# A diffusion layer on one Trainium2 core: norm rows turned by a small matmul before they are written, their reads tied in the queue, and the first operand splits of the up projection behind the last copy of the Fourier part

## The chip, the core and the metric

The kernel runs on one core of one Trainium2 chip. The metric is the device time of one execution in microseconds (us). The text names the engines as the profile does: PE is TensorE (matmuls), DVE VectorE, ACT ScalarE, POOL GpSimd, SP SyncE, whose queue issues nearly all DMA transfers here. "Granted clock" (PEclk) is the share of full TensorE clock that the chip gave: 1.0 is 2.4 GHz, 0.5 is 1.2 GHz.

## The reference, cut to what matters

One layer of a diffusion backbone, in float32, over 2048 tokens of width 1024. `mix` is an output projection of two halves joined: 512 channels of gated retention, and 512 channels of a 2-D Fourier transform.

```python
mix = jnp.concatenate([ret, fourier_mix(f)], axis=-1) @ w_out
x = x + gt_a * rms_norm(mix, g_mix_post)
h_ffn = modulate(rms_norm(x, g_ffn_pre), sh_f, sc_f)
u = h_ffn @ w_up                                    # width 2 * 2816
u = conv3_along_each_row_of_64_tokens(u) + conv_b
a, b = jnp.split(u, 2, axis=-1)
ffn = (jax.nn.silu(a) * b) @ w_down
x = x + gt_f * rms_norm(ffn, g_ffn_post)
```

`rms_norm` divides by the root of the mean square over the 1024 channels: one number for each token, so three norms are to be taken here for each of the 2048 tokens (after `mix`, before the feed-forward part, after it).

## The kernel before, in words

Activations lie with the channels on the 128 partitions and 512 tokens in a row; b = 0 to 3 counts the blocks of 512 tokens, n = 0 to 7 the tiles of 128 channels. Every float32 operand is split in two parts: `split` has ACT cast the high part (L82) and DVE subtract it to get the low part (L83). A product of two split operands is three matmuls (`mm3`, L90, L91, L92).

**Output projection.** `mix_mm(b, n)` runs 32 steps t = 8b + n. The Fourier half is already in SBUF as a tile M; ACT copies it into a PSUM tile `psmix` as a seed (`seed_mix`, L996) two steps ahead (SEEDS = 2), and 12 matmuls with the weights `wr` and the split retention rows `rt` add the other half. ACT copies the sum back into M (L1007) and squares it into `accm`. `load_r` loads and splits the rows `rt` of the next block.

**Norms.** `sum_cols` sums squares over the partitions by 4 matmuls with a column of ones (tile `pc`, L160); DVE scales them (`rp`, L128) and POOL takes the power (L129). The result is 128 x 4: a token is a partition. To multiply a tile that has tokens along the row, the kernel needs it as a row on all partitions. It goes there in one of two ways: `bcast_row` (4 matmuls `pb`, L86, and a copy by ACT, L146), or through DRAM: `row_out` (L133) writes the 128 x 4 tile into a vector of 512, and `row_in` (L138) reads it back, the same 512 numbers on every partition. Eight rows go through DRAM: n1, n2, n3 (before the feed-forward, blocks 1 to 3), m2, m3 (after `mix`) and three of the last norm (`row_f`). Rows `n` come from the sums `accx`, rows `m` from `accm`.

**Between the two.** `mix_post` scales M by the row, adds the residual and squares into `accx`; `x2_cols` and `x2_rows` make the row n. `t_first` and `t_second` then make the right operands of the up projection for blocks 0 and 1 (`h_val`, L1040, and splits `b` and `t`; the last of them are needed some 10 us into the up pass). The dictionary `steps` says after which step t each of these is written in the code.

**Feed-forward.** Two passes over pairs of blocks, each an up projection (tiles `psu`, `psf`) and a down projection (`psd`). Weights come as `ur` (L1152), are summed into `us` for a Strassen-like scheme and split into `u_a`, `u_s`. Blocks 2 and 3 of `mix_post` and `x2_cols` run as a generator, `rest_of_mix`, some of it after each pair of tiles of the first up pass, as "background". At the end of each up pass four tiles `xn` (blocks 1 and 3) are scaled by row n1 or n3.

A scheduler puts the instructions of the program in an order for each engine; an instruction under `keep_in_program_order` stays behind those that were written ahead of it. Each engine then runs its own list strictly in order, and SP issues its DMAs so too.

Of the kernel before, what the change touches and what calls it, by code (L numbers as in the profile page):

```python
# [14 lines left out]
P = 128  # L15
NT = 2048
D = 1024
KT = 8
# [26 lines left out]
J0 = (0, 11), (0,)  # L45
UPJ = [j for k in range(1, KH) for j in (k, k + KH)]
KO = list(range(1, KH)) + [0]
RS = 8, 4
SEEDS = 2
CPAD, APAD, PPAD = 48, 48, 8  # L50
WFN = 272
# [4 lines left out]
def kern(tc, A, out):  # L56
    nc = tc.nc

    with ExitStack() as es:
# [15 lines left out]
        def pmt(shape, name):  # L75
            return psp.tile(shape, F32, tag="pm", name=name, bufs=2)
# [1 line left out]
        def cst(shape, name, p=cp):  # L78
            return p.tile(shape, F32, tag=name, name=name)

        def split(hi, lo, src):
            nc.scalar.copy(hi, src)  # L82
            nc.vector.tensor_tensor(lo, src, hi.bitcast(F32), op=ALU.subtract)  # L83

        def mm(ps, l, r, start, stop):
# [43 lines left out]
            nc.gpsimd.tensor_tensor(o, t[:, 0:n], mhalf[:, 0:n], op=ALU.pow)  # L129

        def row_out(rc, n, name, eng=None):
            d = dp.tile([n * P], F32, tag="row_" + name, name="row_" + name)
            (eng or nc.sync).dma_start(d.rearrange("(i p) -> p i", p=P), rc)  # L133
            return d

        def row_in(rt, d, n, name, eng=None):
            rr = rt([P, n * P], "rr_" + name)
            (eng or nc.sync).dma_start(rr, bass.AP(tensor=d.tensor, offset=d.offset, ap=[[0, P], [1, n * P]]))  # L138
            return rr

        def bcast_row(rt, rc, n, name):
# [870 lines left out]
        def mix_cols(b):  # L1012
            rcm[b] = cst([P, 4], f"rcm{b}", po_)
            sum_cols(accm[b], rcm[b], 4, po_)
            if b > 1:
                rowm[b] = row_out(rcm[b], 4, f"m{b}")

        def mix_rows(b):
            if b < 2:
# [3 lines left out]

        def x2_cols(b):
            sum_cols(accx[b], r2c[:, 4 * b:4 * b + 4], 4, po_)
            if b:
                r2d[b] = row_out(r2c[:, 4 * b:4 * b + 4], 4, f"n{b}")

        def x2_rows(b, eng=None):
            if b > 1 or b in rrn:  # L1030
# [107 lines left out]
        def operands(bb, jobs):  # L1138


            def load(j, one):
                if bb and not one and j in wus:
                    a1, a2, sb = (page([P, KT, P], F32, f"ur{i}") for i in range(3))
                    sa = sump.tile([P, 2, 4, P], F32, tag="sum", name="us")
                    nc.sync.dma_start(a1, A["w_up"][j])
                    nc.sync.dma_start(sa, wus[j][:, 0:2])
                    nc.sync.dma_start(sb, wus[j][:, 2:4].rearrange("p s k c -> p (s k) c"))
                    nc.sync.dma_start(a2[:, 0:4], A["w_up"][j + NJ][:, 4:8])
                    return dict(a11=a1[:, 0:4], a12=a1[:, 4:8], s1=sa[:, 0], s2=sa[:, 1], s4=sb[:, 0:4], s3=sb[:, 4:8], a22=a2[:, 0:4])
                r = [page([P, KT, P], F32, f"ur{i}") for i in range(2)]  # L1150
                for i in range(2):
                    nc.sync.dma_start(r[i], A["w_up"][j + NJ * i])  # L1152
                return dict(a11=r[0][:, 0:4], a12=r[0][:, 4:8], a21=r[1][:, 0:4], a22=r[1][:, 4:8])

            def left_sum(a, o):
                l, r, op = dict(s1=("a21", "a22", ALU.add), s2=("s1", "a11", ALU.subtract),
                                s3=("a11", "a21", ALU.subtract), s4=("a12", "s2", ALU.subtract))[o]
                nc.vector.tensor_tensor(a[o], a[l], a[r], op=op)

            def split_of(a, nme):  # L1160
                w = spt([P, 2, 4, P], f"u_{nme}")
                split(w[:, 0], w[:, 1], a[nme])
                return w

            def gen(nxt):
                held = None
                for i, (j, one) in enumerate(jobs):
                    a = nxt
                    if i + 1 < len(jobs):
                        nxt = load(*jobs[i + 1])  # L1170
                    if one:
                        if held is not None:
                            yield split_of(held, PAIR[6][0])
                            held = None
                        for nme in ONE:
                            yield split_of(a, nme)
                        continue
                    sums = "s1" not in a
                    if sums:
                        sa = sump.tile([P, 2, 4, P], F32, tag="sum", name="us")  # L1180
                        a.update(s1=sa[:, 0], s2=sa[:, 1], s3=a["a21"], s4=sa[:, 1])
                        for o in ("s1", "s2"):
                            left_sum(a, o)
                        if not bb:
                            nc.sync.dma_start(wus[j][:, 0:2], sa)
                    for q, (nme, _) in enumerate(PAIR[:6]):
                        o = dict(s1="s3", a12="s4").get(nme)
                        if sums and o:
                            left_sum(a, o)
                            if not bb:  # L1190
                                nc.sync.dma_start(wus[j][:, ("s4", "s3").index(o) + 2], a[o])
                        yield split_of(a, nme)
                        if q == 1 and held is not None:
                            yield split_of(held, PAIR[6][0])
                    held = a
            return gen(load(*jobs[0]))
# [10 lines left out]
        def at(t, f, *a):  # L1207
            steps.setdefault(t, []).append((f, a))
        for b in range(NB - 1):
            for k in range(4):  # L1210
                at(RS[0] * b + RS[1] * k // 2, load_r, b + 1, k)
        T = {}
        tf, ts = t_first(T, 0), t_second(T, 1)
        T["gen"] = ts
        for b, t in ((0, 9), (1, 17)):
            at(t, mix_cols, b)
            at(t + 1, mix_rows, b)
            for n in range(KT):
                at(t + 2 + n // 2, mix_post, b, n)
            at(t + 6, x2_cols, b)  # L1220
            at(t + 7, x2_rows, b)
        at(27, mix_cols, 2)
        for n in range(KT):
            at(17 + n, next, tf)
        at(26, lambda: up0.append(up_load(0)))
        early = []
        for n in range(4):
            at(28, lambda: early.append(next(up0[0][2])))
        for n in range(12):
            at(26 + n // 2, next, ts)  # L1230
        for t in range(SEEDS):
# [1 line left out]
        for t in range(32):  # L1233
            mix_mm(t // KT, t % KT)
            for f, a in steps.get(t, ()):
                f(*a)


        def rest_of_mix():
            mix_cols(3)  # L1240
            for b in (2, 3):
                mix_rows(b)
                got = mix_load(b, 0)
                yield
                yield
                for n in range(KT):
                    now, got = got, mix_load(b, n + 1) if n + 1 < KT else None
                    mix_post(b, n, now)
                    yield
                for _ in range(XW):  # L1250
                    yield
                x2_cols(b)
                yield

        def conv(y, ps, j):
# [174 lines left out]
        class Norm:  # L1430
# [6 lines left out]
            def f(self, n):  # L1437
                return self.fo[n // 2][:, n % 2]
# [356 lines left out]
```

## Time and profile before

| | |
|---|---|
| device time, median of 3 runs | 2201.43 us (2195.55 to 2203.13) |
| time of the profiled execution | 2195.93 us, of which the span of the trace is 2194.2 |
| mean granted clock | 0.978 |
| PE busy | 2076.4 us, 95% of the span |
| DVE, ACT, POOL busy | 1615.2, 1009.2 and 616.7 us (74%, 46%, 28%) |
| output projection | about 726 to 857 us of the span |
| first up pass, first down pass | 857 to 1311, 1311 to 1521 |
| second up pass, second down pass | 1521 to 1958, 1958 to 2194 |

A row of the timeline gives the start and the length of an instruction or of a run of equal ones, its engine, line, operation and tiles (out<-in), and in brackets how long the engine had stood idle and whom it waited for.

### The profile page before, as it was taken

How to read it: one execution, taken by the hardware profiler on the slowest of the kernel's cores; microseconds unless marked ns; L12 is line 12 of the kernel's file. 1: busy time of each engine (PE TensorE's matmuls, PEld its weight loads, DVE VectorE, ACT ScalarE, POOL GpSimd, SP SyncE). 2: the span in 40 equal slices, each digit the busy share in tenths (PEclk: the TensorE clock that was granted, in tenths of full speed). 3: DMA queues.
4: the chain of work that ended last, by engine and by line, in shares of the span. 5: the costliest groups of instructions: out<-in, count | busy, mean ns of one | idle time of the engine just before them, and what ended most of it. 6: DMA issues, size and time to landing. Idle time of an engine off the chain costs nothing.

```text
span 2194.2 us, 28116 instructions
## 1 busy us (share of the span) xinstructions
PE 2076.4 (95%) x9819; PEld 1711.4 (78%) x9819; DVE 1615.2 (74%) x2346; ACT 1009.2 (46%) x1754; POOL 616.7 (28%) x496
## 2 busy tenths in 40 slices
PE   7899899999899977989989999999999999999996
PEld 3777778888798866778778888887887888878886
DVE  6876877767566387998898886778777777775557
ACT  4342233324444566544545554545555455553441
POOL 4101122323101243242343342021333334331025
PEclk9999999999999988999999999999999999999998
DMA  8676643232562155664564478665355655386653
GB/s 306 213 242 216 192 139 92 100 96 95 146 223 100 52 199 139 183 207 176 183 205 159 154 275 297 218 242 177 135 187 197 185 185 178 135 272 224 200 154 130
DMA packets 202590, 395.20 MB, mean 180 GB/s; under 512 B 31816, under 2 KB 69584, under 8 KB 202448
## 3 DMA queue, kind: packets, MB, share of 16 engines
q1 hardware_dynamic: 194416, 367.07, 51.6%
q0 software_dynamic: 7600, 26.23, 3.3%
q8 instruction: 77, 1.26, 0.2%
q14 instruction: 65, 0.53, 0.1%
q10 hardware_dynamic: 432, 0.11, 0.0%
HBM read 275.33 MB, written 118.00 MB: 179 GB/s over the span
## 4 chain that ended last, share of the span: by engine, by line
PE 56%; DVE 22%; DMA 10%; issue 6%; ACT 3%; POOL 2%; SPq 1%; DVEq 0%; ACTq 0%; POOLq 0%
PE psu L90 8%; PE psu L91 8%; PE psu L92 8%; PE psd L90 5%; PE psd L91 5%; PE psd L92 5%; DMA ur<-in_w_up 2%; DVE u_a L83 2%; DVE y L1259 1%; DVE u_s L83 1%; DVE fd L638 1%; DMA wsum<-in_w_down 1%; DMA adaw<-in_wadaB 1%; PE pada L86 1%; DMA wd<-wsum 1%
## 5 line engine op out<-in xcount | busy, mean ns | idle before, releaser
L83 DVE TENSOR_TENSOR dlo<-draw,dhi 128x1024 fp32r<-128x1024 f32 x154 | 200.3, 1323 | 113.7 <-ACT dhi L82 102.4
L91 PE MATMUL psd<-dlo,dhi 128*128 128x512 f32 (+1 forms) x660 | 247.1, 375 | 2.9 <-DVE dlo L83 2.9
L92 PE MATMUL psd<-dhi,dlo 128*128 128x512 f32 (+1 forms) x660 | 246.2, 375 | 0.0
L1297 POOL TENSOR_TENSOR y<-y,y 128x512 f32<-128x512 f32 x82 | 127.0, 1549 | 388.5 <-DVE y L1260 274.5
L82 ACT CAST dhi<-draw 128x1024 fp32r<-128x1024 f32 x154 | 159.7, 1051 | 162.2 <-PE psd L92 116.5
L90 PE MATMUL psd<-dhi 128*128 128x512 f32 (+1 forms) x660 | 209.4, 375 | 0.6 <-DVE cx L1558 0.6
L91 PE MATMUL psu<-t,u_s 128*128 128x512 f32 x492 | 194.1, 395 | 1.4 <-DVE t L83 1.4
L90 PE MATMUL psu<-t,u_s 128*128 128x512 f32 x492 | 194.9, 396 | 0.0
L92 PE MATMUL psu<-t,u_s 128*128 128x512 f32 x492 | 193.9, 394 | 0.0
L83 DVE TENSOR_TENSOR u_a<-ur,u_a 128x512 fp32r<-128x512 f32 x147 | 139.7, 953 | 61.3 <-ACT u_a L82 60.8
L90 PE MATMUL psu<-b,u_a 128*128 128x512 f32 x424 | 165.6, 391 | 3.1 <-ACT u_a L82 1.9
L91 PE MATMUL psu<-b,u_a 128*128 128x512 f32 x424 | 165.2, 390 | 0.0
L92 PE MATMUL psu<-b,u_a 128*128 128x512 f32 x424 | 165.2, 390 | 0.0
L91 PEld LDWEIGHTS psd<-dlo,dhi 128*128 128x128 f32 x660 | 124.2, 188 | 25.6 <-DVE dlo L83 3.3
L92 PEld LDWEIGHTS psd<-dhi,dlo 128*128 128x128 f32 x660 | 124.2, 188 | 22.3
L90 PEld LDWEIGHTS psd<-dhi 128*128 128x128 f32 x660 | 123.3, 188 | 23.2 <-DVE cx L1558 0.8
L82 ACT CAST u_a<-ur 128x512 fp32r<-128x512 f32 x147 | 90.6, 620 | 103.0 <-PE psu L92 92.3
L1256 ACT ACTIVATE y<-psu,cb,cw 128x512 f32<-128x512 f32 x135 | 104.2, 775 | 19.0 <-DVE psu L1405 13.7
L83 DVE TENSOR_TENSOR u_s<-us,u_s 128x512 fp32r<-128x512 f32 x103 | 84.7, 823 | 38.4 <-ACT u_s L82 38.3
L91 PEld LDWEIGHTS psu<-t,u_s 128*128 128x128 f32 x492 | 94.1, 191 | 22.0 <-DVE t L83 1.9
L90 PEld LDWEIGHTS psu<-t,u_s 128*128 128x128 f32 x492 | 94.1, 191 | 19.9 <-ACT psu L1394 0.9
L92 PEld LDWEIGHTS psu<-t,u_s 128*128 128x128 f32 x492 | 93.8, 191 | 20.0
(438 smaller groups left out, 5313.9 us busy)
## 6 DMA issues: line engine op xcount, KB each, us to landing
ur<-in_w_up SPq DMA_DIRECT2D x74, 512.0 KB, 5.5
draw<-wd SPq DMA_DIRECT2D x88, 256.0 KB, 5.6
draw<-ft SPq DMA_DIRECT2D x88, 256.0 KB, 5.8
ft<-y SPq DMA_DIRECT2D x36, 512.0 KB, 5.5
draw<-in_w_down SPq DMA_DIRECT2D x66, 256.0 KB, 5.1
draw<-fb SPq DMA_DIRECT2D x66, 256.0 KB, 5.3
xt<-in_xT SPq DMA_DIRECT2D x56, 256.0 KB, 4.0
adaw<-in_wadaB SPq DMA_DIRECT2D x24, 512.0 KB, 6.5
```

What stands on the lines that cost most here:

```text
L82: nc.scalar.copy(hi, src)
L83: nc.vector.tensor_tensor(lo, src, hi.bitcast(F32), op=ALU.subtract)
L86: nc.tensor.matmul(ps, l, r, start=start, stop=stop)
L90: nc.tensor.matmul(ps, lhi, rhi, start=start, stop=False, skip_group_check=on)
L91: nc.tensor.matmul(ps, lhi, rlo, start=False, stop=False, skip_group_check=on)
L92: nc.tensor.matmul(ps, llo, rhi, start=False, stop=stop, skip_group_check=on)
L638: tc.keep_in_program_order(nc.vector.tensor_tensor(o_, a_, b_, op=op))
L1256: nc.scalar.activation(y, ps, AF.Identity, bias=cb[:, j:j + 1], scale=cw[:, j, 1:2])
L1259: nc.vector.scalar_tensor_tensor(y3[:, :, 1:64], p3[:, :, 0:63], cw[:, j, 0:1], y3[:, :, 1:64], ALU.mult, ALU.add)
L1297: nc.gpsimd.tensor_tensor(y1, y1, y2, op=ALU.mult)
```

## The change

1. `row_out` first turns the 128 x 4 tile into 4 x 128 by a matmul with the identity (`prow`), DVE copies that out of PSUM (`rowt`), and the DMA writes 4 rows of 128 numbers, where it wrote 512 separate numbers.
2. The reads of `row_in` are tied in program order.
3. `row_out` stands in functions of its own (`mix_out`, `x2_out`), called a step or more after the sums; `rest_of_mix` gets four more yields.
4. `load_r` of block b + 1 stands after steps 8b + 1 to 8b + 4 (before: 8b, 8b + 2, 8b + 4, 8b + 6).
5. `x2_cols` and `x2_rows` stand one step later; the first weights of the up pass (`up_load(0)`) one step earlier.
6. The first four operand splits of the up pass stand two after step 28 and two after step 29, their ACT copies tied; before, all four were written at step 28, free to move.

```diff
-        def split(hi, lo, src):
-            nc.scalar.copy(hi, src)
+        def split(hi, lo, src, tie=False):
+            c = nc.scalar.copy(hi, src)
+            if tie:
+                tc.keep_in_program_order(c)
...
         def row_out(rc, n, name, eng=None):
             d = dp.tile([n * P], F32, tag="row_" + name, name="row_" + name)
-            (eng or nc.sync).dma_start(d.rearrange("(i p) -> p i", p=P), rc)
+            pr = pmt([n, P], "prow")
+            mm(pr, rc, ident, True, True)
+            t = cp.tile([n, P], F32, tag="rowt", name="rowt")
+            nc.vector.tensor_copy(t, pr)
+            (eng or nc.sync).dma_start(d.rearrange("(i p) -> i p", p=P), t)
...
         def row_in(rt, d, n, name, eng=None):
-            (eng or nc.sync).dma_start(rr, bass.AP(...))
+            r = (eng or nc.sync).dma_start(rr, bass.AP(...))
+            tc.keep_in_program_order(r)
...
         def mix_cols(b):
-            if b > 1:
-                rowm[b] = row_out(rcm[b], 4, f"m{b}")
+        def mix_out(b):
+            rowm[b] = row_out(rcm[b], 4, f"m{b}")
...
         def x2_cols(b):
-            if b:
-                r2d[b] = row_out(r2c[:, 4 * b:4 * b + 4], 4, f"n{b}")
+        def x2_out(b):
+            r2d[b] = row_out(r2c[:, 4 * b:4 * b + 4], 4, f"n{b}")
...
-                split(w[:, 0], w[:, 1], a[nme])
+                split(w[:, 0], w[:, 1], a[nme], not bb and len(early) < 4)
...
-                at(RS[0] * b + RS[1] * k // 2, load_r, b + 1, k)
+                at(KT * b + 1 + k, load_r, b + 1, k)
...
-            at(t + 6, x2_cols, b)
-            at(t + 7, x2_rows, b)
+            at(t + 7, x2_cols, b)
+            at(t + 8, x2_rows, b)
+        at(26, x2_out, 1)
         at(27, mix_cols, 2)
+        at(28, mix_out, 2)
...
-        at(26, lambda: up0.append(up_load(0)))
+        at(25, lambda: up0.append(up_load(0)))
         early = []
-        for n in range(4):
-            at(28, lambda: early.append(next(up0[0][2])))
...
             for f, a in steps.get(t, ()):
                 f(*a)
+            if t in (28, 29):
+                early.extend(next(up0[0][2]) for _ in range(2))
...
         def rest_of_mix():
             mix_cols(3)
+            yield
+            mix_out(3)
+            yield
...
                 x2_cols(b)
+                yield
+                x2_out(b)
                 yield
```

The last seeds and the first operand splits in ACT's list, around the last two steps of the output projection; `u_a<-ur` are the splits of the up pass, `psmix<-m` the seed of step 31. Before:

```order
L1007 COPY m_3_5902<-psmix 128x512
L154 ACTIVATE sq<-psmix 128x512
L82 CAST u_a_7299<-ur_7219 128x512
L82 CAST u_a_7302<-ur_7219 128x512
L82 CAST u_a_7305<-ur_7220 128x512
L82 CAST u_a_7308<-ur_7220 128x512
L1041 ACTIVATE h_7311<-h_7311,modB 128x512
L82 CAST t_0_7318<-m_0_5899 128x512
L996 COPY psmix<-m_3_6094 128x512
```

The same place in the changed kernel:

```order
L1014 COPY m_3_5902<-psmix 128x512
L161 ACTIVATE sq<-psmix 128x512
L81 CAST t_0_7310<-m_0_5899 128x512
L1003 COPY psmix<-m_3_6094 128x512
L1014 COPY m_3_5966<-psmix 128x512
L1050 ACTIVATE h_7303<-h_7303,modB 128x512
L1014 COPY m_3_6030<-psmix 128x512
L1050 ACTIVATE h_7304<-h_7304,modB 128x512
L81 CAST b_1_7315<-h_7304 128x512
L81 CAST u_a_7322<-ur_7198 128x512
L81 CAST u_a_7325<-ur_7198 128x512
```

Four splits stood ahead of the last seed; now the seed stands ahead of all of them, and PE's first three `psu` matmuls, which stood ahead of step 31, stand behind it. SP's list at the end of the first up pass, where the row n1 is read (`fb<-y` are stores of the gated tiles, `wu` stores of weight sums, `ur` loads of weights). Now:

```order
L1200 DMA wu_225<-us 128x512
L1161 DMA ur_10345<-in_w_up 128x1024
L1161 DMA ur_10346<-in_w_up 128x1024
L1293 DMA ft_0_194<-y_9864 128x1024
L1194 DMA wu_227<-us 128x1024
L1200 DMA wu_227<-ur_10346 128x512
L1293 DMA fb_0_151<-y_10170 128x512
L144 DMA rr_n_10657<-row_n_7221 128x512
L1200 DMA wu_226<-us 128x512
```

Before, the same read stood in SP's list at the end of the output projection, between the writes of rows n1 and m2 and the first weights:

```order
L133 DMA row_n_7144<-r2c 128x4x1
L1152 DMA ur_7219<-in_w_up 128x1024
L1009 DMA x_2_3_119<-m_3_6030 128x512
L1152 DMA ur_7220<-in_w_up 128x1024
L133 DMA row_m_7263<-rcm_7254 128x4x1
L1009 DMA x_3_3_123<-m_3_6094 128x512
L957 DMA xt_7798<-in_xT 128x512
L138 DMA rr_n_10637<-row_n_7144 128x512
L1152 DMA ur_7295<-in_w_up 128x1024
L1009 DMA x_4_3_127<-m_3_5902 128x512
```

The read moved by some 400 us, to just before the tile that uses it. DVE's list follows it: the four scalings `xn<-xn,rr_n`, which stood in the middle of the first up pass, now stand at its end, between the work on the outputs `psu` and `psf`. Now:

```order
L1275 SCALAR_TENSOR_TENSOR y_10321<-psu,cw,y_10321 128x8x63
L1049 SCALAR_TENSOR_TENSOR xn<-xn,a_5852,rr_n_10657 128x512
L1276 SCALAR_TENSOR_TENSOR y_10321<-psu,cw,y_10321 128x8x63
L138 COPY rowt<-prow 4x128
L1421 TENSOR_TENSOR psu<-psu,x_10323 128x512
L84 TENSOR_TENSOR u_s_10465<-us,u_s_10465 128x512
L1049 SCALAR_TENSOR_TENSOR xn<-xn,a_5852,rr_n_10657 128x512
L1275 SCALAR_TENSOR_TENSOR y_10321<-psu,cw,y_10321 128x8x63
L1424 TENSOR_TENSOR psf<-psu,x_10323 128x512
```

The same tiles before (their numbers differ by 6, since the program has a few tiles more now):

```order
L1259 SCALAR_TENSOR_TENSOR y_10315<-psu,cw,y_10315 128x8x63
L1260 SCALAR_TENSOR_TENSOR y_10315<-psu,cw,y_10315 128x8x63
L1405 TENSOR_TENSOR psu<-psu,x_10317 128x512
L83 TENSOR_TENSOR u_s_10445<-us,u_s_10445 128x512
L1259 SCALAR_TENSOR_TENSOR y_10315<-psu,cw,y_10315 128x8x63
L1260 SCALAR_TENSOR_TENSOR y_10315<-psu,cw,y_10315 128x8x63
L1408 TENSOR_TENSOR psf<-psu,x_10317 128x512
```

Two `xn` and a `rowt` now stand ahead of `psf`, the tile that the next matmuls are given.

## Rows read from the trace of the kernel before

**Rows 1.** The page: the span, the busy time of each engine, and the issues of weight loads `ur`: how many, KB each, us from issue to landing (median).

```profile
span 2194.2 us, 28116 instructions
PE 2076.4 (95%) x9819; PEld 1711.4 (78%) x9819; DVE 1615.2 (74%) x2346; ACT 1009.2 (46%) x1754; POOL 616.7 (28%) x496
...
ur<-in_w_up SPq DMA_DIRECT2D x74, 512.0 KB, 5.5
```

**Rows 2.** What PE waited for from 690 to 920 us, three of the answers: total us, times, longest.

```profile
PE pc L160 <- DVE accx L155: 4.1, 1, 4.1
PE psmix L91 <- DVE rt L83: 3.5, 2, 2.7
PE psmix L90 <- ACT rt L82: 3.2, 1, 3.2
```

**Rows 3.** Timeline of PE at the end of the output projection: step 30 ends with the first row, step 31 are the rows from 851.17 to 856.03.

```profile
839.36 0.39 PE L92 MATMUL psmix<-rt,wr 128*128 128x512 f32 x1
841.14 0.50 PE L90 MATMUL psu<-b,u_a 128*128 128x512 f32 x1 [1.39 <-ACT u_a L82]
...
851.17 0.80 PE L90 MATMUL psmix<-rt,wr 128*128 128x512 f32 x1 [8.80 <-ACT psmix L996]
...
856.03 0.43 PE L92 MATMUL psmix<-rt,wr 128*128 128x512 f32 x1
856.30 0.40 PE L90 MATMUL psu<-b,u_a 128*128 128x512 f32 x1
```

**Rows 4.** Timeline of SP and ACT at the same place: the write of row n1 and the issue of the first weight load; the four splits and the seed of step 31.

```profile
826.48 0.37 SPq L133 DMA_DIRECT2D row_n<-r2c  x1
826.95 0.46 SPq L1152 DMA_DIRECT2D ur<-in_w_up  x1
...
840.47 1.14 ACT L82 CAST u_a<-ur 128x512 fp32r<-128x512 f32 x2 [3.53 <-DMA ur<-in_w_up]
848.36 1.14 ACT L82 CAST u_a<-ur 128x512 fp32r<-128x512 f32 x2 [6.75 <-DMA ur<-in_w_up]
...
850.53 0.58 ACT L996 COPY psmix<-m 128x512 f32<-128x512 f32 x1
```

**Rows 5.** Timeline of PE earlier in the output projection: the second wait for the last rows `rt` of block 3 and the matmuls behind it, then the sums and the row of block 1.

```profile
816.45 0.80 PE L91 MATMUL psmix<-rt,wr 128*128 128x512 f32 x1 [2.72 <-DVE rt L83]
...
821.31 0.63 PE L91 MATMUL psmix<-rt,wr 128*128 128x512 f32 x1
...
824.14 0.95 PE L160 MATMUL pc<-ones,accx 128*128 128x1 f32 x8
...
826.51 1.16 PE L86 MATMUL pb<-ident,r2c 128*128 128x128 f32 x8 [0.85 <-POOL r2c L129]
```

**Rows 6.** Busy time by windows: start and end, length, then PE, its weight loads, DVE, ACT, POOL (instructions in brackets), the granted clock, DMA share, GB/s.

```profile
787.79:821.34 33.55, 27.65 (x119) 22.26 (x118) 32.26 (x42) 24.98 (x46) 14.77 (x8) 0.91 0.59 196
821.34:885.10 63.76, 51.35 (x221) 40.87 (x219) 46.01 (x67) 39.12 (x70) 21.34 (x11) 0.89 0.53 133
1200.00:1260.00 60.00, 60.00 (x269) 49.37 (x268) 49.97 (x67) 29.27 (x50) 18.27 (x13) 1.00 0.46 153
```

**Rows 7.** Timeline of DVE from 820 to 886 us: the last `accx` of block 1 and the scaling of its sums, the splits that waited, and the operand `t` that PE waited for.

```profile
820.66 0.68 DVE L155 TENSOR_TENSOR accx<-accx,sq 128x512 f32<-128x512 f32 x1
825.20 0.16 DVE L128 TENSOR_SCALAR rp<-pc 128x4 f32<-128x4 f32 x1 [3.86 <-PE pc L160]
...
841.12 1.29 DVE L83 TENSOR_TENSOR u_a<-ur,u_a 128x512 fp32r<-128x512 f32 x2 [1.72 <-ACT u_a L82]
849.01 1.29 DVE L83 TENSOR_TENSOR u_a<-ur,u_a 128x512 fp32r<-128x512 f32 x2 [6.60 <-ACT u_a L82]
...
884.43 0.68 DVE L83 TENSOR_TENSOR t<-h,t 128x512 fp32r<-128x512 f32 x1
```

**Rows 8.** Timeline of PE: the wait for that operand.

```profile
885.16 0.50 PE L91 MATMUL psu<-t,u_s 128*128 128x512 f32 x1 [1.44 <-DVE t L83]
```

**Rows 9.** Timeline of PE and DVE where the four `xn` of block 1 stand before: two of them, and PE's wait behind them, with the matmuls that follow it.

```profile
1140.44 1.40 DVE L1040 SCALAR_TENSOR_TENSOR xn<-xn,a,rr_n 128x512 f32<-128x512 f32 x1 [0.58 <-DMA xn<-x]
...
1143.47 1.77 DVE L1040 SCALAR_TENSOR_TENSOR xn<-xn,a,rr_n 128x512 f32<-128x512 f32 x1
...
1153.21 0.79 PE L90 MATMUL psu<-t,u_a 128*128 128x512 f32 x1 [5.21 <-DVE psf L1408]
...
1156.36 0.46 PE L91 MATMUL psu<-t,u_s 128*128 128x512 f32 x1
```

**Rows 10.** Timeline of SP, DVE and PE where the `xn` of block 1 stand in the changed kernel: the store after which the row is read, the places of the first `xn` and of `psf`, and the matmul that is given `psf`.

```profile
1245.26 0.32 SPq L1277 DMA_DIRECT2D fb<-y  x1
...
1247.07 0.74 DVE L1260 SCALAR_TENSOR_TENSOR y<-psu,cw,y 128x504 f32<-128x504 f32 x1
...
1250.70 0.69 DVE L1408 TENSOR_TENSOR psf<-psu,x 128x512 f32<-128x512 f32 x1
...
1251.45 0.50 PE L90 MATMUL psu<-t,u_a 128*128 128x512 f32 x1
```

**Rows 11.** DMA to landing, in us, least, median and most: of the eight row writes, then of the nine row reads (n3 is read twice).

```profile
DMA to landing us min/median/max: 8.4/10.0/17.1
DMA to landing us min/median/max: 4.0/5.7/13.8
```

**Rows 12.** Timeline of POOL at the last row: its power.

```profile
2121.59 2.00 POOL L129 TENSOR_TENSOR rcf<-rp,mhalf 128x4 f32<-128x4 f32 x1 [6.62 <-DVE rp L128]
```

More of the change, by code (lines that the diff above doesn't have):

```diff
@@ L47 @@
 KO = list(range(1, KH)) + [0]
-RS = 8, 4
 SEEDS = 2
@@ L137, in row_in @@
             rr = rt([P, n * P], "rr_" + name)
-            (eng or nc.sync).dma_start(rr, bass.AP(tensor=d.tensor, offset=d.offset, ap=[[0, P], [1, n * P]]))
+            r = (eng or nc.sync).dma_start(rr, bass.AP(tensor=d.tensor, offset=d.offset, ap=[[0, P], [1, n * P]]))
+            tc.keep_in_program_order(r)
             return rr
```

## The prediction, made before the changed kernel ran

> **What bounds the kernel now.** The page comes first: PE is busy 2076.4 of 2194.2 us [rows 1], so all its idle time together is 118 us, and an edit of this kind pays only where PE stands still or runs at half clock. The normal pace is read from a stretch without idle time: 269 PE instructions in 60.00 us, 0.22 us each, at a granted clock of 1.00 [rows 6].
>
> Next, what PE waits for around the output projection. The longest wait is for the seed of step 31: 8.80 us, just after a wait of 1.39 for the first `psu` [rows 3]. The 12 matmuls of step 31 then take 851.17 to 856.30, 5.1 us, where 12 x 0.22 = 2.7 would do [rows 3, 6]: after the idle time they run at the lower of the two clock levels. ACT tells why the seed was late: four splits stood ahead of it and waited 3.53 and 6.75 us for loads `ur` [rows 4]. The first of these loads was issued at 826.95, right behind the write of row n1, and released ACT at 840.47, 13.5 us later [rows 4]; the median of such loads is 5.5 [rows 1]. The row writes themselves land 8.4 to 17.1 us after issue, though each is only 2 KB [rows 11].
>
> Then the other waits there: 3.2 and 2.7 us for the last rows `rt` of block 3, and 4.1 for `accx` of block 0 [rows 2].
>
> Last, DVE, which feeds all this. From 787.79 to 821.34 it is busy 32.26 of 33.55 us: it has no slack until the last `accx` of block 1 is there. From there to the operand `t` that PE waits for (end 885.1) it is busy 46.01 of 63.76 [rows 6, 7].
>
> **The change part by part.** The sum is made against the profiled execution's own 2195.93 us; the median of the runs lies 5.5 above that.
>
> *The seed ahead of the splits.* Gone are 1.39 + 8.80 us of waiting and 5.1 - 2.7 = 2.4 of half clock: 12.6 us of PE time. The three `psu` matmuls that filled the gap only move behind step 31.
>
> *`rt` earlier.* Gone are 3.2 + 2.7 us and the slow matmuls behind them: the 12 that start from 816.45 to 821.31 come at 0.44 us [rows 5], which costs 12 x 0.22 = 2.6. That is 8.5, but most of it is given back at once. The sums of block 1 (`pc<-accx`) start at 824.14 [rows 5], and they need the `accx` that DVE finishes at 821.34 with no slack [rows 6, 7]. PE gets there 8.5 earlier, less five matmuls that now stand in between (1.1): at 816.7. It waits 4.6 us for DVE, as it does for block 0 (4.1) [rows 2], and a few matmuls behind the wait run slow again. The sums start at 821.4 to 823.4, as DVE's own start in this stretch may come up to 2 us later (the sums of block 0 also stand one step later). Against 824.14 + 1.1 that is a gain of 1.8 to 3.8, less about 1.5 of half clock: I take 2.
>
> PE therefore ends the output projection 12.6 + 2 = 14.6 us earlier, at 841.7 instead of 856.30.
>
> *Where the stall goes.* Now `t` is late. DVE's idle time before it is 63.76 - 46.01 = 17.8 us. The two waits for splits, 1.72 + 6.60 = 8.3 [rows 7], go with the tied splits, and with them about 1 of the small waits that follow; those around row n1 (3.86 and others [rows 7]) stay, as its chain of sum, power, row and copy is the same. So `t` is ready at 885.1 - 9.3 = 875.8. PE would be there at 885.16 - 1.44 - 14.6 = 869.1 [rows 8] and waits 6.7 instead of 1.44. The stage gains 9.3 and not 14.6; a slow stretch behind the longer wait takes about 0.5 more than today's. I take **-9**. Bounds: -14.6 if DVE keeps up; -4 if half of DVE's idle time stays because the splits wait at their new place for loads as late as before.
>
> *Writes by matmul.* No row shows a `prow`. Its nearest row is `pb`: 512 columns in 1.16 us [rows 5], so 128 columns take 0.29; eight of them 2.3, of which five stand where PE is the bound: **+1.5**. The copy `rowt` is like `rp`, 0.16 us [rows 7], eight in 2300 us, hidden in DVE's idle time. What a faster write is worth is bounded by who waits for it: the loads beside it (in the term above). The last row has its `prow` only two matmuls behind the sums; the power takes until 2121.59 + 2.00 = 2123.6 [rows 12], where PE today has been through ten others. PE stands still for about 1.8 us. The row then lands earlier, which may return some of it at the tail: **+1** (bounds -1.5 and +2.5).
>
> The Trainium skill, "TensorE: Matmul & The Clock Gate", part 2 (step by step), says that the matmuls stay in program order, only weight loads being pulled ahead; by that a `prow` that waits for POOL holds all the work behind it. No row here has such a matmul, though `pb` waited 0.85 us for POOL in just this way.
>
> *Tied reads.* Row n1 was read in advance; now its read follows the store that is issued at 1245.26 today [rows 10], and lands 4.0 to 5.7 us later [rows 11]: at 1249.6 to 1251.3. The first `xn` stands ahead of the output row at 1247.07 [rows 10]. DVE, strictly in order, waits 2.5 to 4.2 us there. Two `xn` (0.75 each without contention) and a `rowt` also stand ahead of `psf`, whose end at 1251.39 is today just in time for the matmul at 1251.45 [rows 10]. PE stalls 4.2 to 5.9 us and runs slow behind that for 1.5: **+6.5**. On the other side the `xn` leave the middle of the pass, where two of them cost DVE 1.40 + 1.77 and a wait of 0.58, 3.75 together, ahead of a `psf` for which PE waited 5.21, its next matmuls being at half clock (7 in 3.15 us instead of 1.6) [rows 9]: **-4.7**, leaving 1.5 of the wait. In the second pass I expect the read in time: **-0.5** for a stall of the same kind that goes. Together +1.3 (bounds -5 and +5).
>
> The Trainium skill, "DMA: Bandwidth & Descriptors", rules for kernel authors, would have the transfer issued early and its semaphore waited for late, so that the fixed cost overlaps with work; the tie does the opposite. By the rows above that is the +6.5; nothing was seen to wait for this read before.
>
> **Sum:** -9 + 1.5 + 1 + 1.3 = -5.2 on the profile; I add -1 for row m3, whose slow write also shares the queues with the first weight sums, and -1 for the shorter landing of loads beside n2, n3 and the rows f, both estimates without a row of their own. -7.2 gives 2188.7 for a profiled execution, 2194.2 for the median.
>
> **Rivals.** A change of 0.3%, 6.6 us, is about what a measurement of this kernel can tell from none.
>
> - *DVE keeps up.* The tied splits also spread ACT and DVE work, and `t` comes by 870. For it: 17.8 us of DVE idle time in the stretch [rows 6]. Against it: 46 us of DVE work between row n1 and `t`, with PE needing 48. Then the stage gives -14.6, the sum is -12.8: median 2188.5. Chance 0.2.
> - *Loads as late as before.* If the loads are late because of other traffic and not the element-wise row writes, the first splits wait at their new place, and the stage gives -4: sum -2.2, median 2199. For it: two writes alone, at 2 KB each, lie beside the loads. Against: 13.5 us where the median is 5.5. Chance 0.23.
> - *Slower: a tied read late.* There are two such reads at the ends of the up passes. One read today took 13.8 us to land [rows 11]. At that price DVE waits 12.3 us, not 3.3, and the stall is 9 longer; in both passes it is 18 and more, with 2 us of clock. Sum -7.2 + 20 = +13, median 2214; with one of them late, +2, 2203. It decides once the two waits together exceed the forecast by 14. For it: the stores around the read (`fb`, `wu`, `ur`) fill the queues, and DVE is in order. Against: the median of 5.7. Chance of a result slower by over 0.3%: 0.13.
> - *The write is no faster.* Nothing waits for the turned rows sooner than 20 us after, except the last; then the sum loses its -2 and up to 1 more at the tail: 2197. It is part of the second case.
>
> **How the numbers follow.** The sum as it stands has 0.44, with a range of its own of 2190 to 2198. Faster by over 0.3% means a median under 2194.8: all of the first rival and a little over half of the likeliest, 0.2 + 0.27 = 0.47, and 0.03 of the second, 0.50. Slower than 2208: 0.13, and 0.37 lie between. The range leaves out a tenth at each end: below, the best of the first rival; above, the late reads: 2183 to 2206.
>
> **What would show it.** Right: step 31 without a wait for its seed; PE waits 4 to 6 us for `accx` of block 1 and 5 to 8 for a `t` near 870 to 876; `psf` at the end of the first up pass waits 4 to 6 us behind the first `xn`; the stall at 1153 is under 2.5; the row writes land in under 6 us. Wrong: an `xn` that waits over 10 us; splits that wait for `ur` as before; `prow` rows with several us of idle time before them.

## The result, and the profile after

The changed kernel takes 2182.76 us (median of 5 runs, 2181.33 to 2189.29) against 2197.65 for the kernel before run beside it (5 runs, 2195.55 to 2203.13): a ratio of 0.9933, 95% interval 0.9918 to 0.9948. Run again later it gave 0.9946 (0.9930 to 0.9963). The forecast was 2194.2, range 2183 to 2206: the direction was right, the gain twice the forecast, and the time lies just below the range. Part of the miss is the base: I set the median 5.5 us above the profiled execution, as the three runs before stood; with more runs the median before fell to 2197.65, and the changed kernel's median lies 1.4 above its profiled 2181.33. The rest, 14.6 us of profiled time against 7.2 forecast, is of the sum.

The page of the changed kernel, to be held against [rows 1]:

```profile
span 2179.6 us, 28163 instructions
PE 2073.0 (95%) x9835; PEld 1706.8 (78%) x9835; DVE 1613.7 (74%) x2354; ACT 1008.4 (46%) x1754; POOL 625.3 (29%) x496
```

What PE waited for from 690 to 920 us, against [rows 2, 3]:

```profile
PE pc L167 <- DVE accx L162: 9.0, 2, 5.1
PE psu L91 <- ACT psu L1410: 1.7, 1, 1.7
PE psu L92 <- DVE t L84: 1.4, 1, 1.4
...
PE psmix L91 <- ACT psmix L1003: 0.6, 1, 0.6
```

The 8.80 us for the seed and both waits for `rt` are gone. A second wait for `accx` has come (3.92 of the 9.0), as forecast. The wait for `t` is 1.42 us, not 6.7; just ahead of it stands a new one of 1.71 for a copy of `psu` by ACT, 3.1 in all.

SP's row writes and first weight loads in the changed kernel, and the landing of all eight writes, against [rows 4, 11]:

```profile
822.46 0.85 SPq L1161 DMA_DIRECT2D ur<-in_w_up  x2
829.01 0.33 SPq L139 DMA_DIRECT2D row_n<-rowt  x1
...
838.43 0.27 SPq L139 DMA_DIRECT2D row_m<-rowt  x1
841.90 0.93 SPq L1161 DMA_DIRECT2D ur<-in_w_up  x2
...
DMA to landing us min/median/max: 2.6/2.6/2.6
```

A turned row lands in 2.6 us each time, where the element-wise one took 8.4 to 17.1. The Trainium skill, "DMA: Bandwidth & Descriptors", specifications, asks for at least 512 bytes in a transfer if it is to run at full rate, and says that below this the DMA engines read, modify and write. The sizes here, 4 bytes against 512, and the two landings agree with the direction of that rule; the reading and modifying itself is seen in no run here.

DVE and PE at the end of the first up pass, against [rows 10]:

```profile
1236.40 0.75 DVE L1049 SCALAR_TENSOR_TENSOR xn<-xn,a,rr_n 128x512 f32<-128x512 f32 x1 [3.70 <-DMA rr_n<-row_n]
...
1241.16 0.50 PE L91 MATMUL psu<-t,u_a 128*128 128x512 f32 x1 [2.93 <-DVE psf L1424]
```

DVE waits 3.70 us for the tied read (forecast 2.5 to 4.2), and PE behind it 2.93 for `psf` (forecast 4.2 to 5.9). The stall of 5.21 us in the middle of the pass [rows 9] is 2.54 in the changed kernel (forecast 1.5):

```profile
1136.34 0.50 PE L91 MATMUL psu<-t,u_a 128*128 128x512 f32 x1 [2.54 <-DVE psf L1424]
```

### The profile page after: what moved, and what is told of

It reads as the page before. It is cut to its first block, busy times and chain, and to the rows that moved or that the text cites. A ratio compares the mean times of both kernels' runs of the same rounds, so it can differ in the third digit from the quotient of the medians.

```text
span 2179.6 us, 28163 instructions
## 1 busy us (share of the span) xinstructions
PE 2073.0 (95%) x9835; PEld 1706.8 (78%) x9835; DVE 1613.7 (74%) x2354; ACT 1008.4 (46%) x1754; POOL 625.3 (29%) x496
## 4 chain that ended last, share of the span: by engine, by line
PE 59%; DVE 21%; DMA 7%; issue 6%; ACT 4%; POOL 2%; SPq 1%; DVEq 0%; ACTq 0%; POOLq 0%
PE psu L91 8%; PE psu L92 8%; PE psu L93 8%; PE psd L91 6%; PE psd L92 5%; PE psd L93 5%; DVE u_a L84 2%; DVE y L1275 2%; DVE u_s L84 2%; DMA wsum<-in_w_down 1%; PE pada L87 1%; DVE fd L645 1%; DMA fr<-fscr 1%; DMA wd<-wsum 1%; PE psk L93 1%
```

## The experiments

The runs are compared in two ways. The ratio, with its interval, is taken from all the runs of a kernel and of the kernel before, run beside it on the same chip; it differs a little from the ratio of the medians. Behind it stand landmarks of the profiles: the start of an instruction less the start of the sums of block 0 (`pc<-accx`, 781.87 in the kernel before), and that against the kernel before, in us; minus is earlier. (These sums themselves start at 780.3 to 787.3 in the 14 profiles, so times are counted from them.) `t` is the operand of [rows 8], psf 2 is the second of 41 `psf` (920.38 before), psf 13 the one at 1152.46, psf 17 at 1231.53, psf 18 at 1250.70 [rows 10], psf 41 at 1945.15.

| kernel | ratio to before (95%) | t | psf 2 | psf 13 | psf 17 | psf 18 | psf 41 | end |
|---|---|---|---|---|---|---|---|---|
| changed | 0.9933 (0.9918 to 0.9948) | -9.7 | -11.4 | -18.0 | -16.0 | -11.4 | -12.8 | -15.8 |
| changed, again | 0.9946 (0.9930 to 0.9963) | -9.7 | -11.5 | -18.4 | -16.3 | -11.8 | -9.2 | -12.2 |
| splits alone | 1.0000 (0.9986 to 1.0015) | -2.0 | -2.4 | -3.4 | -2.6 | -1.3 | -2.7 | -2.9 |
| rt alone | 1.0004 (0.9986 to 1.0022) | -2.1 | -2.8 | -1.6 | -0.4 | -0.1 | 0.0 | 0.2 |
| turned write alone | 0.9972 (0.9959 to 0.9985) | -8.0 | -7.1 | -5.1 | -2.5 | -2.5 | -3.0 | -6.0 |
| no splits, no rt | 0.9945 (0.9923 to 0.9967) | -9.8 | -10.7 | -17.0 | -14.9 | -10.9 | -9.8 | -12.9 |
| old write, all rows | 0.9983 (0.9969 to 0.9998) | -7.7 | -7.7 | -15.3 | -13.2 | -5.2 | -7.1 | -7.7 |
| old write, n1 and m2 | 0.9939 (0.9924 to 0.9954) | -8.4 | -11.2 | -17.7 | -15.7 | -11.6 | -10.3 | -13.3 |
| old write, m3 and n3 | 0.9968 (0.9955 to 0.9980) | -9.5 | -9.0 | -15.9 | -13.7 | -6.1 | -2.7 | -5.7 |
| old write, last row | 0.9952 (0.9935 to 0.9968) | -9.7 | -11.5 | -17.8 | -15.6 | -11.0 | -9.5 | -8.9 |
| untied reads | 0.9946 (0.9929 to 0.9963) | -9.0 | -10.8 | -17.7 | -11.8 | -11.8 | -9.3 | -11.3 |
| early reads | 0.9952 (0.9935 to 0.9969) | -8.9 | -10.7 | -17.3 | -15.2 | -15.4 | -10.3 | -11.1 |
| early read, pass 0 | 0.9926 (0.9907 to 0.9944) | -9.7 | -11.5 | -17.8 | -15.5 | -15.7 | -12.3 | -15.3 |

The first two rows are the same program: up to psf 18 they agree within 0.4 us, behind it they differ by up to 3.6. So a few us in the later columns, or at the end of one profile, prove nothing; the columns up to psf 18 and the stalls do.

### Parts of the change on the kernel before

Splits alone (with `split(..., tie)` as in the change), then rt alone; turned write alone is `row_out` as in the change and all else as before.

```diff
-        for n in range(4):
-            at(28, lambda: early.append(next(up0[0][2])))
...
+            if t in (28, 29):
+                early.extend(next(up0[0][2]) for _ in range(2))
...
-                at(RS[0] * b + RS[1] * k // 2, load_r, b + 1, k)
+                at(KT * b + 1 + k, load_r, b + 1, k)
```

> The kernel before with one part of the change alone: the first four operand splits stand two after step 28 and two after step 29, their ACT copies tied behind the last seed. Theory of the prediction (the operand t, made by DVE, becomes the bound): step 31 has no wait for its seed, t is ready near 876 to 878 where it was 885.2, PE waits 4 to 6 us for it, and the end comes 7 to 9 us earlier (about 2188 to 2190 against 2195.9 for a profiled execution). Rival 1 (DVE keeps up): 12.6 us earlier, about 2183. Rival 2 (the loads are late behind the element-wise write of row n1, which is kept here): the first splits wait several us for ur at their new place, 4 us or less are won, 2192 or later.

> The kernel before with one part alone: the rows rt of block b + 1 are loaded and split after steps 8b + 1 to 8b + 4. Theory of the prediction: the waits of 3.2 and 2.7 us for rt are gone, a wait of 4 to 6 us for the accx of block 1 takes their place, and at most 2 us are left, none at the end (2194 to 2196 against 2195.9), because the seed of step 31 still waits for the same loads. Rival (PE keeps what it wins): 8.5 us earlier, 2187.

> The kernel before with one part alone: rows are turned by prow, copied by rowt and written as 4 rows of 128; splits, rt, ties and the places of the calls as before. Theory of the prediction's sum: prow costs 2.5, faster writes give 2: within 2 us of before (2194 to 2198 for a profiled execution). Rival, from the earlier runs (the stage lost 5 us when only the element-wise write came back): the write is itself the cause of the late loads; the loads ur beside it land in 5 to 7 us and not 13 to 18, the wait of 8.8 us for the seed of step 31 shrinks to under 3 though four splits still stand ahead of it, the tail is 2.5 shorter, and the end comes 8 us or more earlier (2188 or less).

Splits alone and rt alone give nothing that the times show, and 2 us at `t`. In the first the seed is no longer late, but ACT and DVE now wait at the splits' new place, as the second rival of its expectation had it (timeline of ACT and DVE, splits alone):

```profile
855.10 1.89 ACT L82 CAST u_a<-ur 128x512 fp32r<-128x512 f32 x3 [7.36 <-DMA ur<-in_w_up]
...
855.75 0.69 DVE L85 TENSOR_TENSOR u_a<-ur,u_a 128x512 fp32r<-128x512 f32 x1 [4.81 <-ACT u_a L82]
...
858.33 0.69 DVE L1039 TENSOR_TENSOR t<-h,h 128x512 f32<-128x512 f32 x1 [1.89 <-ACT h L1043]
```

DVE's wait for the splits has moved, not gone, and `t` is made by DVE. With rt alone the waits for `rt` became waits for `accx` (6.7 us in all, where it was 4.1) and seeds (4.3). Nothing is won at the end, as expected, but not for the reason given: the seed of step 31 waits 1.8 us there and not 8.80, and `t` comes only 2.1 earlier. The 8.80 us stood in front of a `t` that was late anyway.

The turned write alone, with four splits still ahead of the seed, does what the reorder was to do. ACT and SP of that kernel:

```profile
824.51 0.38 SPq L1156 DMA_DIRECT2D ur<-in_w_up  x1
828.44 0.32 SPq L137 DMA_DIRECT2D row_n<-rowt  x1
830.77 0.37 SPq L1156 DMA_DIRECT2D ur<-in_w_up  x1
...
839.63 2.17 ACT L82 CAST u_a<-ur 128x512 fp32r<-128x512 f32 x4
842.22 0.59 ACT L1000 COPY psmix<-m 128x512 f32<-128x512 f32 x1
```

The four splits run back to back without a wait (3.53 and 6.75 us in [rows 4]), the seed is copied at 842.22 where it was 850.53, and no wait for it is left. `t` comes 8.0 us earlier. The cause lies in the transfers. The loads `ur` that were issued between 820 and 846 us took this long to land, first the four of the kernel before, then three of the four here (the trace lacks the landing of one):

```profile
DMA to landing us min/median/max: 10.8/14.1/18.6
```

```profile
DMA to landing us min/median/max: 3.3/4.5/5.1
```

Turning also moves the write behind the first load in SP's list (824.51 and 828.44, where it was 826.95 and 826.48), and that order may be part of the gain; no run parts the two. But the load issued right behind the turned row m2, at 835.82, lands in 5.1 us too. A window of 12 us in each kernel, with a write of n1, one of m2 and two issues of `ur` in it, shows the same (columns as in [rows 6]; the last three are granted clock, DMA share, GB/s):

```profile
826.00:838.00 12.00, 11.49 (x59) 9.78 (x59) 8.57 (x13) 8.71 (x17) 7.28 (x6) 1.00 0.41 21
```

```profile
827.00:839.00 12.00, 10.51 (x54) 8.35 (x55) 7.10 (x12) 8.23 (x16) 5.71 (x5) 1.00 0.51 157
```

In the 12 us around and after the element-wise write of row n1 the DMA engines moved 21 GB/s, though they were busy 41% of the time; with the turned row 157. Of the 8 us at `t`, 5.5 are given back by psf 17; what takes them I did not settle. The gain is 0.28%, 6 us, all the same, 3 of them behind psf 41.

### The changed kernel without the reorder

```diff
-                split(w[:, 0], w[:, 1], a[nme], not bb and len(early) < 4)
+                split(w[:, 0], w[:, 1], a[nme])
...
-                at(KT * b + 1 + k, load_r, b + 1, k)
+                at(8 * b + 2 * k, load_r, b + 1, k)
...
-        at(25, lambda: up0.append(up_load(0)))
+        at(26, lambda: up0.append(up_load(0)))
+        for n in range(4):
+            at(28, lambda: early.append(next(up0[0][2])))
...
-            if t in (28, 29):
-                early.extend(next(up0[0][2]) for _ in range(2))
```

> The changed kernel with the order of the splits and of the rows rt undone (four splits at step 28, free; load_r at steps 8b, 8b + 2, 8b + 4, 8b + 6; up_load(0) at step 26); turned writes, tied reads and moved calls kept. Theory (the two cures replace each other: with fast writes the loads come in time whatever stands ahead of the seed): step 31 has no wait for its seed over 1 us, t comes 1 to 2.5 us later than in the changed kernel, and so does the end: ratio to before 0.994 to 0.9955. Rival, the prediction's step (the order of the splits is worth the most): 4 us or more slower than the changed kernel, ratio over 0.9955.

> The changed kernel itself, run again beside the next two on one chip. Expected of every theory: a ratio of 0.992 to 0.995 to the kernel before; the first operand t ready 7 to 10 us earlier than before, counted from the first matmul of the Fourier mix that waits (693.8 us before).

Run beside each other the two have ratios of 0.9945 and 0.9946, and `t` within 0.1 us. The 1 to 2.5 us that I expected the reorder to keep did not show: the order of splits, seeds and rows `rt` is worth nothing that can be measured once the writes are turned (the intervals are some 4 us to either side). The two are cures for one wait: with the old writes the reorder does help (`t` at -7.7 in the next run, where splits or rt alone give 2), where the first loads, with `up_load(0)` a step earlier, are issued in pairs at 825.6 and 838.5 and no longer one by one until 844.1. That this is how it helps is read from the issues and was not tried by itself.

This leaves a gap: turned write alone has 0.9972, the changed kernel without the reorder 0.9945 and without the tie (below) 0.9946. The intervals overlap a little, but psf 13 stands at -17.0 and -17.7 there, against -5.1. So some 6 us come from what is left, the moved calls and the added yields (part 3 of the change and the rest of part 5). No run has these alone: that they bring it is argued from what was taken out, not shown.

### The old write in the changed kernel

First all rows; then the old line for named rows alone (n1 and m2, m3 and n3, or the last).

```diff
-            pr = pmt([n, P], "prow")
-            mm(pr, rc, ident, True, True)
-            t = cp.tile([n, P], F32, tag="rowt", name="rowt")
-            nc.vector.tensor_copy(t, pr)
-            (eng or nc.sync).dma_start(d.rearrange("(i p) -> i p", p=P), t)
+            (eng or nc.sync).dma_start(d.rearrange("(i p) -> p i", p=P), rc)
...
+            if name in ("m3", "n3"):
+                (eng or nc.sync).dma_start(d.rearrange("(i p) -> p i", p=P), rc)
+                return d
```

> The changed kernel with the element-wise row writes of before (512 separate numbers from 128 x 4), without prow and rowt; all else as changed. Theory of the prediction's sum: prow costs 1.5 on PE and 1 at the last row, what the fast writes give back elsewhere is 2: within 2 us of the changed kernel (2180 to 2184). Rival, from the trace of the changed kernel: the fast writes are worth far more than they cost, 3 us at the tail, where POOL gets its row some 10 us earlier, and 2 to 6 us where the loads ur lie beside the writes of n1 and m2: 2186 to 2191, with the stalls of 1.25 and 1.67 us of the last 50 us back.

> The changed kernel with the element-wise write for rows n1 and m2 alone, the two that are issued while the first weights of the up pass load. Theory (these two writes hold up the loads and stores beside them): the start of the first up pass comes 3 to 5.5 us later than in the changed kernel, and most of it stays to the end: 2184 to 2187, the tail as in the changed kernel. Rival (the gain lies in the other six writes): within 1 us of the changed kernel there and at the end.

> The changed kernel with the element-wise write for the last row alone. Theory: POOL gets that row some 10 us later, its multiplications then fall beside DVE's last splits and additions, the stalls of 1.2 and 1.7 us return, and the end comes 2.4 to 3.5 us later, all of it in the last 60 us. Rival, the prediction's term (the prow that waits for POOL costs more than the early row brings): 0 to 1 us earlier, as the wait of 0.8 us at prow goes.

> The changed kernel with the element-wise write for rows m3 and n3 alone. Theory (these two hold up what the engines wait for: m3 the first weight sums, n3 the tied read of row n1 issued 3 us behind it): the second psf of the first up pass comes about 2 us later against the changed kernel, counted from the first psf; DVE waits 7 to 8 us for the read of n1 where it waited 3.70; psf behind it waits 6 to 7 us; the kernel loses 4 to 6 us against the changed one (ratio 0.996 to 0.9975 to before). Rival (the loss of 7 to 9 us with all old writes is spread over all eight): under 2.5 us lost, the read waited for as in the changed kernel.

With all old writes the ratio goes from 0.9933 and 0.9946 to 0.9983: the turned writes are worth 8 to 11 us (0.0037 to 0.0050 of 2197). I had put them at 2 for prow's 2.5.

Where it lies: rows n1 and m2 alone, 1.3 us at `t`, gone by psf 2, and no change of the ratio; the 3 to 5.5 that I expected of them did not come. Rows m3 and n3 carry more, 0.9968 against 0.9933 and 0.9946, 5 to 8 us (the interval overlaps that of the second). Row n2 and the first two rows f were not tried by themselves. DVE in that kernel, at the start of the up pass and at its end, then PE:

```profile
900.13 0.69 DVE L1170 TENSOR_TENSOR us<-ur 128x512 f32<-128x512 f32 x1 [4.18 <-DMA wu<-us]
...
1241.30 0.75 DVE L1052 SCALAR_TENSOR_TENSOR xn<-xn,a,rr_n 128x512 f32<-128x512 f32 x1 [7.30 <-DMA rr_n<-row_n]
...
1245.87 0.79 PE L91 MATMUL psu<-t,u_a 128*128 128x512 f32 x1 [6.50 <-DVE psf L1427]
```

Row m3's write holds up a store of weight sums, whose buffer DVE waits for (4.18; no such wait in the changed kernel). A store `fb` issued 1.5 us behind that write lands in 13.2 us; behind the turned one it takes 2.0. Row n3's write is issued 3.3 us ahead of the tied read of row n1, and the read is waited for 7.30 us and not 3.70. In the changed kernel the turned n3 is issued 6.7 us behind that read, so here too the order is part of it. Step psf 17 to 18 costs 7.6 to 8.1 with these old writes, 4.0 to 4.6 without. The tie is dearer with the old writes; the turned writes do not need the tie (next section).

The last row, 2.4 to 3.6 us by the landmarks: from psf 41 to the end its kernel loses 0.6, and the one with all old writes gains 0.6, where the changed one gains 3.0 in both its profiles. The times alone do not part the two (0.9952 against 0.9933 and 0.9946), and with untied and with early reads the turned last row gains only 2.0 and 0.8 there, PE waiting 0.8 for a split again. POOL with the old last write, then in the changed kernel:

```profile
2114.22 0.84 POOL L136 DMA_DIRECT2D row_f<-rcf  x1 [0.29 <-POOL rcf L130]
2124.41 0.55 POOL L147 DMA_DIRECT2D rr_f<-row_f  x1 [9.35 <-DMA row_f<-rcf]
2130.72 2.64 POOL L1495 TENSOR_TENSOR cs<-cs,rr_f 128x512 f32<-128x512 f32 x2 [5.76 <-DMA draw<-fb]
```

```profile
2112.05 0.60 POOL L139 DMA_DIRECT2D row_f<-rowt  x1 [1.05 <-DVE rowt L138]
2114.89 0.56 POOL L144 DMA_DIRECT2D rr_f<-row_f  x1 [2.25 <-DMA row_f<-rowt]
2119.02 8.77 POOL L1492 TENSOR_TENSOR cs<-cs,rr_f 128x512 f32<-128x512 f32 x2 [3.56 <-DMA rr_f<-row_f]
```

POOL starts to apply the row 7.0 us after its write was issued, and not 16.5. With the old write the multiplications fell beside DVE's last splits: two of these took 4.47 us there, and PE waited 1.03 and 0.60 for splits; in the changed kernel the first two multiplications are done by 2127.8, the same splits take 1.47 and 1.23 each, and PE has no such wait. The `prow` that I feared cost 0.79 us:

```profile
2111.05 0.38 PE L87 MATMUL prow<-ident,rcf 128*4 128x128 f32 x2 [0.79 <-POOL rcf L130]
```

### The tie of the reads

Untied (the first line alone); then, with the tie of the read kept, the read called one pair of tiles earlier (in both passes, and in the last run in the first alone, as shown), and the scaling of `xn` tied so that it stays in the last pairs.

```diff
-            tc.keep_in_program_order(r)
...
+                if j == twos[-2] and not bb:
+                    x2_rows(b1)
...
+                tc.keep_in_program_order(h)
```

> The changed kernel with the row reads not tied in program order; they move forward in the queues again, and so do the four xn of block 1, some 70 DVE instructions. Theory of the prediction: the tied read costs 4.6 us at the end of the first up pass (DVE waited 3.70 us for it, the end of the pass moved from -14.9 to -10.3 against before), and its move out of the middle is worth 2.7: without the tie about 2 us faster than the changed kernel (2179), with no wait of DVE for rr_n. Rival (the tie is part of the gain, as the xn fall into stretches where DVE has no slack): 2 us or more slower, 2183 to 2187, the psf stalls in the middle of the pass longer.

> The changed kernel with the read of rows n1 and n3 called one pair of tiles (some 20 us) before the last pair, and the four xn tied so that they stay in the last pair. Theory: DVE does not wait for the read (it waited 3.70 us), psf at the end of the first up pass comes 3.5 to 4.5 us earlier, and the end too: about 2177 for a profiled execution, the fastest so far. Rival (the two xn and the rowt ahead of psf are what costs): under 1 us is won.

> The changed kernel with the read of row n1 one pair of tiles earlier and its four xn tied to the last pair, in the first pass alone (in the second pass, where the same tie made a stall of 1.87 us into 3.66, all is as changed). Theory: the wait of 3.70 us goes, psf at the end of the first pass moves by 2 to 4 us, and the kernel is 2 to 3 us faster than the changed one run beside it (ratio lower by 0.001 to 0.0015). Rival (the xn and the rowt themselves cost it): same within 1 us.

Untied, the read and the `xn` move forward, DVE waits for no row, and the 4.6 us between psf 17 and 18 are gone. But the `xn` come back into the pass 70 instructions earlier and cost 4 us there (psf 14 to 15), so psf 18 stands where it stood, and the ratio is that of the changed kernel: neither the 2 us won of the theory nor the 2 us lost of its rival. The middle of the pass, psf 2 to 13, gains 6 to 8 us in every kernel made from the changed one, with or without the tie or the turned write, and 1.0 at most with one of the three parts alone; the `xn` are out of the stretch ahead of psf 13 in all of them. The step into psf 13, where two `xn` stood, gains 2.6 to 2.7 of it; the rest lies in the steps ahead of it, among which background work now stands a pair of tiles later.

Read early but with `xn` kept in the last pairs, the step from psf 17 to 18 is -0.2 (4.6 with the tie alone). In the second pass the same tie made a stall of 1.87 into 3.66 us, and the kernel was no faster (0.9952), against the fastest that I expected. With the early read in the first pass alone the kernel takes 2178.37 us against 2184.21 for the changed one beside it, 0.9926 against 0.9946. It is the fastest measured; the intervals overlap, so that it beats the changed kernel is likely, not shown.

## Why the prediction was right or wrong, point by point

The forecast by stretches, against the table (changed kernel, first profile):

| stretch | forecast | measured |
|---|---|---|
| to `t` | -9 | -9.7 |
| `t` to psf 2 (row m3) | -1 | -1.7 |
| psf 2 to 17 (`xn` out of the middle) | -4.7 | -4.6 |
| psf 17 to 18 (tied read) | +6.5 | +4.6 |
| psf 18 to 41 (second pass, other rows) | -1.5 | -1.4 |
| psf 41 to the end (last row) | +1 | -3.0 |
| `prow`, within these stretches | +1.5 | counted above |
| ahead of the sums of block 0 | 0 | +1.2 |
| all | -7.2 | -14.6 |

The fifth row proves nothing: in the second profile of the same program it is +2.6.

- **The worth of the faster write: wrong, and the step that failed.** The prediction has "What a faster write is worth is bounded by who waits for it: the loads beside it (in the term above)", and prices the writes at +1.5 on PE, +1 at the last row and -2 for row m3 and the rest. With the old writes put back the changed kernel loses 8 to 11 us, 2.0 of them at `t`, in the term above; beside that term some -6 to -9 was due where the sum has +0.5. A `prow` is two matmuls, 0.38 us together, where 0.29 was reckoned; the cost was about right. What the neighbours of a write gain was missed: the loads, the stores and the tied read beside it, and POOL at the tail.
- **The last row, +1: the largest part of that miss.** The `prow` waited 0.79 us (reckoned 1.8), but the early row is worth 2.4 to 3.6 at the end by the landmarks. The bound of -1.5 was too near: I looked at the landing alone, not at what POOL's multiplications collide with.
- **The seed ahead of the splits, 12.6 us of PE time, and "the two waits for splits, 1.72 + 6.60 = 8.3, go with the tied splits": wrong as a cause.** Tied splits alone leave DVE 4.81 and 1.89 us of waiting; without them the changed kernel is as fast. What made the splits late was the element-wise write in the same queue. I had the rows for it (13.5 us for a load whose median is 5.5, 8.4 to 17.1 for 2 KB [rows 1, 4, 11]); the rival "Loads as late as before" named it, but only as the case in which little is won. The size, -9 against -9.7, came out because the turned writes are in the same change: in part that is luck.
- **What bounds the stage: right in the main.** `t`, made by DVE, sets the start of the up pass, and it starts at 875.93 where it was to be ready at 875.8. A second wait for `accx` came, 3.92 us where 4.6 was reckoned. PE stood still for 3.1 us at `t` and the copy ahead of it, where 6.7 was reckoned.
- **Tied reads, +6.5 at the new place: right in place and cause, too large by 2.** DVE waited 3.70 (2.5 to 4.2 reckoned), PE 2.93; the step costs 4.6. PE did not run slow behind the wait: the next matmuls come every 0.23 us. The rule of the Trainium skill ("DMA: Bandwidth & Descriptors", rules for kernel authors: issue early, wait late) agrees with the early read at this place: the step from psf 17 to 18 falls from 4.6 to -0.2.
- **The `xn` out of the middle, -4.7: right in kind, the size by luck.** The stall that was to shrink from 5.21 to 1.5 is 2.54, and the step into psf 13 gains 2.7. The other 3.9 us between psf 2 and 13 had no term (background work stands a pair of tiles later there; that this brings them was not tried), and 2.0 us are lost again by psf 17. That the net is -4.6 is chance.
- **Rival "DVE keeps up" (2188.5):** its time is nearest to the measured one, its reason did not hold: DVE stayed the bound, with fewer waits. **"Loads as late as before":** this came with the splits alone, not in the changed kernel. **"A tied read late":** it did not happen here, but it does with the old write of n3 ahead of it (7.30 us). **"The write is no faster":** it is, 2.6 us.

## What to carry to other kernels

The writes of 512 separate 4-byte numbers were paid for here by their neighbours, since little waited for what they wrote. Look for loads and stores beside such a write that land late, and cost the write by them. When one wait has two possible cures, price each with the other one present. And when a stalled engine is followed by another late operand, a gain there is only as long as the next one's lateness; follow the engine that makes it (here DVE), not the one that shows the wait.

## What was not expected of the hardware

- Around an element-wise write of 2 KB the core's DMA moved 21 GB/s for 12 us, at a DMA share of 0.41, and the four 512 KB loads issued behind it took 10.8 to 18.6 us to land; with the turned rows it was 157 GB/s and 3.3 to 5.1 us.
- The same 2 KB in runs of 512 bytes lands in 2.6 us, eight times of eight.
- Two profiles of the same program, laid on each other at the sums of block 0 (783.0 and 781.1 us), agree within 0.4 us for the next 450 us and then part by up to 3.6 us.
